# Values of the sample kept per pair of heads, and chunks of keys taken with a step

## The chip, the cores and the metric

The kernel runs on one core of a Trainium2 chip, as one launch. The metric is the device time of that launch in microseconds; of the kernel before there are three timed runs, 959.19, 959.48 and 960.69 us, and their median, 959.48 us, is the time that counts. One more execution was profiled. All times inside the kernel come from that execution.

The engines are named as the profile names them: PE multiplies matrices, PEld loads its weights (the stationary operand, one column after the other), DVE, ACT and POOL work on elements, SP issues nearly all DMAs. A DMA moves packets: runs of bytes that are contiguous on both sides.

## The reference

One encoder layer is applied to a prompt of 256 tokens and to a sample of 2048 tokens. The tokens are laid out as rows of 64 on a grid. Half of the layer is a neighbourhood attention with 8 heads of 64, the other half a Fourier mix; both are normalised, gated and projected.

```python
def encoder_layer(x, w_in, rpb, w_fourier, b_fourier, g_pre, g_na, g_f, w_out, g_post):
    h = rms_norm(x, g_pre)
    proj = h @ w_in
    q, k, v, z_a, u_f, z_f = jnp.split(proj, [...], axis=-1)
    y_a = neighbourhood_attention(q, k, v, rpb)
    y_f = fourier_mix(u_f, w_fourier, b_fourier)
    mixed = jnp.concatenate([rms_norm(y_a, g_na) * jax.nn.silu(z_a),
                             rms_norm(y_f, g_f) * jax.nn.silu(z_f)], axis=-1)
    out = mixed @ w_out
    return x + rms_norm(out, g_post)
```

In the attention a query sees 8 rows by 16 columns of keys around it (in the prompt, which has only 4 rows, all 4). Everything is float32.

## The kernel before

**Stages.** From 0 to about 548 us the projections run. Float32 products are made of three products of float32r halves (a high and a low part; the helper `mm3`, L163). From 548 to 600 us come the Fourier transform's small matrices. From 600 to 843 us runs the attention, mixed with the Fourier half of the output projection. From 843 us the attention half of the output projection runs over 18 tiles.

**Where v goes.** The values v come out of the projection as tiles of 128 tokens by 512 columns (8 heads of 64). `put_rows` (L359) stores a tile of the sample to `vN` in DRAM, which is indexed by half of the columns, grid row, column, and the 512 channels. `v_copy` (L366) copies parts of `vN` to the four tensors `vD`, one for each strip of 23, 31, 31 or 24 columns of keys (`KW`, L32), so that the keys of one strip and some neighbouring grid rows lie one behind the other. The prompt's values go to `vP` directly.

**The groups of the attention.** `G` (L1261) holds 36 groups: for each of 4 pairs of heads (`pr`) the prompt and then, for 4 bands of grid rows (`R`, with 11, 15, 15 and 12 rows of keys, `NR`) and two halves of the columns (`hc`), 256 queries in two tiles `b` of 128. Each tile has its own strip of keys, so n = rows times strip width keys: 253 to 465 in the sample, 160 in the prompt.

**A group's way.** `prep_v` (L1183) loads the values of the pair's two heads: it cuts the n keys into m chunks of z keys (m is 2 to 4), and puts key number j*z + p on partition p, chunk j, of the tile `v` ([128, 7, 128]). One DMA loads all chunks of a tile, or two where the last chunk is shorter than the memory behind it allows. z is rounded up to a multiple of 8. `scores` (L1211) makes the logits, `bias_max` (L1237) adds the bias and finds the maximum, `exps` (L1250) and `soft` (L1254) make probabilities `w`, [128 queries, 2 heads, n keys]. `transp` (L1571) turns them, chunk by chunk: the chunk of `w` is the stationary operand, the identity (128 columns) moves, and the result in `ptb` has keys on partitions. ACT and DVE copy `ptb` to `pt`. `pv` (L1586) multiplies `v` and `pt`, chunk by chunk, into one accumulator. The chunks' list, `g["ch"]`, has for each chunk its first key, its number of keys and its place in `v`.

**What sets the order.** The program's order is written by hand; each engine runs its instructions in that order. In step k of the loop at L1816, `scores` works on group k, `transp` and `pv` on group k - 1, `prep_v` (near the step's end) on group k + 1, and `prep` (its queries) on group k + 4. So the values loaded at the end of step k are read by `pv` near the end of step k + 2. SP issues DMAs in order, and each of them waits until the eighth before it has landed, since they take turns on eight semaphores.

**The instructions that matter here.** In one pass over the pairs, `transp` makes, per head, 3 tiles of 2 chunks, 11 of 3 and 4 of 4: 55 transposes. With 2 heads and 4 pairs these are 440. Their chunks have 80 to 128 columns, and the columns of one chunk lie one behind the other in `w`.

Of the kernel before, what the change touches and what calls it, by code (L numbers as in the profile page):

```python
# [10 lines left out]
F32 = mybir.dt.float32  # L11
# [19 lines left out]
K0 = (0, 4, 12, 20)  # L31
KW = (23, 31, 31, 24)  # L32
# [142 lines left out]
def build(tc, A, O):  # L175
    nc = tc.nc
# [3 lines left out]
    dr = es.enter_context(tc.tile_pool(name="dr", bufs=1, space=DRAM))  # L180
# [1 line left out]
    qD = dr.tile([4, 128, T], F32, name="qD")  # L182
    kD = dr.tile([4, 128, T], F32, name="kD")

    vD = [dr.tile([32, w, 512], F32, name="vD%d" % i) for i, w in enumerate(KW)]
    vP = dr.tile([2, 4, 40, 512], F32, name="vP")
    zD = dr.tile([2, 512, T], F32, name="zD")
    ZD = dr.tile([128, 16, 512], F32, name="ZD")
    uD = dr.tile([TP, 512], F32, name="uD")

    vN, uN = [dr.tile([2, 32, 32, 512], F32, name=n) for n in ("vN", "uN")]
    sD = dr.tile([5, 128, 4, 512], F32, name="sD")
    xD = dr.tile([7, 128, 4, 512], F32, name="xD")
    ivD = dr.tile([18, 128], F32, name="ivD")
# [5 lines left out]
    ident = cst.tile([128, 128], F32, name="ident")  # L200
# [24 lines left out]
    def mmt(n):  # L225
        x = mmc[0] % 5 > 2
        mmc[0] += 1
        return ps.tile([128, n], F32, tag="t" if x else "a", name="mm", bufs=2 if x else 3)
# [115 lines left out]
    def vu_out(m, c):  # L344
        s, b = PL[c]
        o = st.tile([128, 512], F32, tag="f", name=m + "o", bufs=3)
        x = row_tile(c)
        nc.scalar.activation(o, acc.pop((m, c)), AF.Copy, scale=invt[:, x:x + 1])
        if s is not None:
            put_rows(m, 0, b, s, o)  # L350
        elif m == "u":
            nc.sync.dma_start(uD[c * 128:c * 128 + 128, :], o)
        else:
            for r in range(4):
                nc.sync.dma_start(vP[c, r, 8 * c:8 * c + 32], o[32 * r:32 * r + 32])
                x = 24 * (1 - c)
                nc.sync.dma_start(vP[1 - c, r, 32 * c:32 * c + 8], o[32 * r + x:32 * r + x + 8])

    def put_rows(m, sg, b, s, o):  # L359
        r = 16 * sg + 4 * s  # L360
        nc.sync.dma_start((vN if m == "v" else uN)[b, r:r + 4].rearrange("r c e -> (r c) e"), o)


    VC = ((0, 0, 0, 23, 0), (1, 0, 8, 24, 0), (1, 1, 0, 7, 24), (2, 0, 24, 8, 0), (2, 1, 0, 23, 8), (3, 1, 8, 24, 0))

    def v_copy(i):  # L366
        x, b, c0, n, d0 = VC[i]
        nc.sync.dma_start(vD[x][:, d0:d0 + n], vN[b][:, c0:c0 + n])


    uu_ = {}
# [125 lines left out]
    def vu(sg, S, hooks):  # L497
# [7 lines left out]
        for i, (j, s) in enumerate(seq):  # L505
            for x in loads.get(i, ()):
                op_load(x)
            if i in splits:
                op_split(splits[i])
            for f in hooks.get(i, ()):  # L510
                f()
            p = mmt(512)
            h, l = op_[j]
            th, tl = bnew[sg, j]
            for k in range(4):
                mm3(nc, p, th[:, k, 128 * s:128 * s + 128], tl[:, k, 128 * s:128 * s + 128], h[k // 2][:, k % 2],
                    l[k // 2][:, k % 2], k == 0, k == 3)
            T2 = lambda o, a: nc.vector.tensor_tensor(out=o, in0=a, in1=p, op=ALU.add)
            if j == 0:
                uc[s] = et("uc")  # L520
                nc.scalar.copy(uc[s], p)
            elif j == 2:
                T2(uc[s], uc[s])
            elif j == 3:
                u4[s] = et("u4")
                T2(u4[s], uc[s])
            else:
                o = st.tile([128, 512], F32, tag="f", name="vuo", bufs=3)
                T2(o, (u4 if j in (4, 6) else uc)[s])
                if j == 4:  # L530
                    T2(uc[s], uc[s])
                put_rows("v" if j in (1, 6) else "u", sg, int(j in (4, 6)), s, o)
# [104 lines left out]
    for kp in range(4):  # L637
        ks = slice(2 * kp, 2 * kp + 2)
        v = part(RV[kp // 2], kp)
# [131 lines left out]
    for b in range(16):  # L771
# [13 lines left out]
        if 2 <= b < 8:  # L785
            x, y = divmod(b, 2)
# [9 lines left out]
        p = mmt(512)[:, :TP]  # L796
# [3 lines left out]
        o = st.tile([128, 256], F32, tag="f", name="f", bufs=3)  # L800
        if kind % 2:
            i, d = p, o
        else:
            i = p.rearrange("p (b r c) -> p b r c", b=2, c=32)
            d = o.rearrange("p (r b c) -> p b r c", b=2, c=32)
# [47 lines left out]
    for i in range(16):  # L853
        sg, pr = divmod(i, 8)
# [14 lines left out]
        o = [st.tile([128, 1024], F32, tag="f", name="f", bufs=3) for x in range(2)]  # L869
# [31 lines left out]
        for j in range(7):  # L901
            for f, d in ((u_load, 0), (u_split, 4), (u_stage1, 6)):
                x = 7 * pr + j - 7 - d
# [33 lines left out]
            if sg == 0:  # L937
                x, y = divmod(7 * (pr - 1) + j, 14)
# [27 lines left out]
            if 9 <= i < 15 and j == 2:  # L966
                v_copy(i - 9)
            p = mmt(512)
# [34 lines left out]
    ptb = [ps.tile([128, 512], F32, tag="t", name="ptb", bufs=2) for i in range(2)]  # L1003
# [179 lines left out]
    def prep_v(g):  # L1183
        cs = slice(g["pr"] * 128, g["pr"] * 128 + 128)
        g["v"] = jl.tile([128, 7, 128], F32, tag="v", name="v", bufs=VB)
        g["ch"], j = [], 0
        for b, (c0, w) in enumerate(g["t"]):
            n = g["nr"] * w
            src = (vP[b] if g["R"] is None else vD[2 * g["hc"] + b][K0[g["R"]]:]).rearrange("r c e -> (r c) e")
            m = -(-n // 128)  # L1190
            z = min(-(-n // m) + 7 & ~7, 128)
            f = m if src.shape[0] >= m * z else n // z
            nc.sync.dma_start(g["v"][:z, j:j + f], src[:z * f, cs].rearrange("(j p) e -> p j e", p=z))
            if f < m:
                nc.sync.dma_start(g["v"][:n - z * f, j + f], src[z * f:n, cs])
            ch = [(z * x, min(z, n - z * x), j + x) for x in range(m)]
            g["ch"].append(ch)
            j += len(ch)
        g["za"] = jl.tile([128, 256], F32, tag="za", name="za", bufs=VB)
        nc.sync.dma_start(g["za"], zD[1, cs, g["ts"]])  # L1200

# [69 lines left out]
    for g in G[:2]:  # L1271
        prep(g)
        prep_v(g)
# [11 lines left out]
    for t, (g, x) in enumerate(zip(G, (0, 640))):  # L1285
        g["w"] = []
        for c0, w in g["t"]:
            n = 2 * g["nr"] * w
# [282 lines left out]
    def transp(g, b):  # L1571
        ch = g["ch"][b]
        n, z = len(ch) * 128, ch[0][1]
        o = jp.tile([128, 2, 512], F32, tag="pt", name="pt", bufs=PB)
        for h in range(2):
            for j, (c0, nk, v) in enumerate(ch):
                nc.tensor.transpose(ptb[h][:nk, j * 128:j * 128 + 128], g["w"][b][:, h, c0:c0 + nk], ident)  # L1577
            if h == 0:
                nc.scalar.copy(o[:z, h, :n], ptb[h][:z, :n])  # L1579
            else:  # L1580
                V.tensor_copy(o[:z, h, :n], ptb[h][:z, :n])
        g["pt"] = g.get("pt", []) + [o]
# [109 lines left out]
    def part(P, name, n):  # L1692
        return [sm.tile([128, n, 128], F32R, tag="y%s%d" % (x, n) if n < 4 else "y" + x, name="y" + x,
                        bufs=3 if n == 4 else 1) for x in "hl"]
# [103 lines left out]
    prep(G[4])  # L1798
    f_mm(0)
    transp(G[0], 0)  # L1800
    f_norm(range(2))
    transp(G[0], 1)
    soft(G[1], 1)
    run_later()
# [4 lines left out]
    pv(G[0])  # L1809
    ys_load(ftiles[2])  # L1810
    prep_v(G[2])
    split_q(G[3])
    prep(G[5])
    ones32 = sm.tile([128, 32], F32, name="ones32", bufs=1)
    nc.vector.memset(ones32, 1.0)
    for k in range(2, len(G) + 1):  # L1816
        pr, i = divmod(k, 9)
        g, f = G[k] if k < len(G) else None, G[k - 1] if k else None
# [14 lines left out]
        if k == 28:  # L1833
            for c, x in enumerate(("kh", "kl")):
                w = kp.tile([128, T], F32R, tag=x, name="wk")
                WO[c] = [w[:, 56 + D * y:56 + D * y + D] for y in range(2)]
        if k in WK:
            c, y = WK[k]
# [3 lines left out]
        x = k // 2 + 1  # L1842
# [11 lines left out]
        if not g:  # L1854
            a_mm(atiles[0], 0, range(6))
        transp(f, 0)
        if g:
            exps(g, 0, 1)
# [57 lines left out]
        if k + 1 < len(G):  # L1916
            prep_v(G[k + 1])
# [123 lines left out]
```

## Time and profile before

| what | us |
|---|---|
| median of three runs | 959.48 |
| the profiled execution | 958.19 |
| its span, first to last instruction | 956.4 |
| PE busy | 944.8 |
| PEld busy | 784.3 |
| DVE busy | 732.0 |
| ACT busy | 505.8 |
| POOL busy | 453.3 |

The granted clock of PE was 0.997 of full speed. The DMA queue that SP feeds moved 270.68 MB. PE's matmuls overlap each other at their ends, so the durations of single matmuls are longer than the time from one to the next; how often they start is read from a row that merges several. A weight load overlaps the matmul before it.

### The profile page before, as it was taken

Reading aid. Unit: us, or ns where it says so; the run is one execution under the profiler, and the core shown is the slowest. Engines: PE = TensorE matmul, PEld = TensorE weight load, DVE = VectorE, ACT = ScalarE, POOL = GpSimd, SP = SyncE. Lnnn points to the kernel's source line nnn. Section 1 sums busy time; section 2 is a strip of 40 time slices with the busy share of each in tenths; the row PEclk is TensorE's granted clock in tenths of the full one; section 3 lists DMA queues with packets and bytes.
Section 4 is the critical chain, followed back from the end, with each engine's and each line's share of the span. In section 5 each row is a group of like instructions: output and inputs, shape, how many; then the busy total and the mean of one; then the engine's idle time right before and its main releaser. Section 6 shows DMA issues by size and latency. Waiting matters only on the chain.

```text
span 956.4 us, 16730 instructions
## 1 busy us (share of the span) xinstructions
PE 944.8 (99%) x5595; PEld 784.3 (82%) x5595; DVE 732.0 (77%) x1347; ACT 505.8 (53%) x1088; POOL 453.3 (47%) x426
## 2 busy tenths in 40 slices
PE   9999999999999999999999999999999999999996
PEld 7889988888888888888888879788787888788885
DVE  6758987788876765698887369777888878759876
ACT  6835676433334532233344267677876777654443
POOL 4100002464751302575566045567899798624444
PEclk9999999999999999999999999999999999999998
DMA  9899697557848894499889996698998999889995
GB/s 356 298 385 336 243 339 270 189 201 270 299 188 323 314 341 144 175 352 361 300 289 338 338 341 246 215 276 281 309 253 253 290 280 312 239 296 327 305 317 197
DMA packets 140790, 272.17 MB, mean 285 GB/s; under 512 B 12854, under 2 KB 80664, under 8 KB 137440
## 3 DMA queue, kind: packets, MB, share of 16 engines
q1 hardware_dynamic: 140352, 270.68, 82.9%
q8 instruction: 45, 0.74, 0.3%
q10 hardware_dynamic: 288, 0.40, 0.1%
q14 instruction: 41, 0.34, 0.1%
q0 software_dynamic: 64, 0.02, 0.0%
HBM read 181.37 MB, written 96.81 MB: 291 GB/s over the span
## 4 chain that ended last, share of the span: by engine, by line
PE 89%; DMA 4%; DVE 2%; POOL 2%; ACT 1%; issue 1%; SPq 0%; DVEq 0%; POOLq 0%; ACTq 0%
PE mm L166 18%; PE mm L164 18%; PE mm L165 18%; PE po L1504 10%; PE ptb L1577 5%; PE pv L1593 5%; PE s L1225 4%; DMA yr<-yD 2%; PE px L1689 2%; PE pz L1689 2%; DMA yo<-xt 1%; PE py L164 1%; PE py L165 1%; PE py L166 1%; PE ptb L1043 1%
## 5 line engine op out<-in xcount | busy, mean ns | idle before, releaser
L164 PE MATMUL mm<-xh,wa 128*128 128x512 f32 x448 | 174.4, 389 | 0.0
L166 PE MATMUL mm<-xh,wa 128*128 128x512 f32 x448 | 174.3, 389 | 0.0
L165 PE MATMUL mm<-xl,wa 128*128 128x512 f32 x448 | 174.3, 389 | 0.0
L545 POOL TENSOR_TENSOR ws<-wr 128x512 f32<-128x512 f32 x16 | 22.6, 1415 | 219.3 <-DMA wr<-wz 215.6
L1259 POOL TENSOR_SCALAR w<-w,m 128x465 f32<-128x465 f32 (+9 forms) x136 | 89.3, 670 | 32.7 <-DVE m L1256 13.5
L165 PEld LDWEIGHTS mm<-xl,wa 128*128 128x128 f32 x448 | 84.1, 188 | 17.5
L164 PEld LDWEIGHTS mm<-xh,wa 128*128 128x128 f32 x448 | 84.1, 188 | 17.5
L166 PEld LDWEIGHTS mm<-xh,wa 128*128 128x128 f32 x448 | 84.1, 188 | 17.4
L560 DVE TENSOR_TENSOR wa<-wr,wa 128x512 fp32r<-128x512 f32 x60 | 75.4, 1264 | 21.9 <-ACT wa L559 21.6
L1504 PE MATMUL po<-wk,yh 128*128 128x512 f32 x280 | 87.1, 392 | 0.9 <-ACT yh L1490 0.9
L1252 ACT ACTIVATE w<-w,m 128x465 f32<-128x465 f32 (+9 forms) x136 | 78.4, 579 | 14.3 <-DVE m L1247 13.6
L1968 POOL TENSOR_TENSOR xt<-of,xt 128x512 f32<-128x512 f32 x34 | 43.2, 1293 | 54.6 <-issue 33.0
L1247 DVE CUSTOM_DVE_ANT_1 w<-s,tb 128x465 f32<-128x465 f32 (+8 forms) x124 | 61.4, 529 | 8.9 <-PE s L1225 8.0
L598 POOL TENSOR_TENSOR mt<-mt,rmask 128x880 f32<-128x880 f32 (+2 forms) x24 | 50.3, 2111 | 32.6 <-DVE mt L594 26.2
L164 PE MATMUL mm<-vh,xh 128*128 128x512 f32 x168 | 65.4, 389 | 0.0
L165 PE MATMUL mm<-vl,xh 128*128 128x512 f32 x168 | 65.4, 389 | 0.0
L166 PE MATMUL mm<-vh,xl 128*128 128x512 f32 x168 | 65.4, 389 | 0.0
L1504 PEld LDWEIGHTS po<-wk,yh 128*128 128x128 f32 x280 | 52.1, 188 | 12.2 <-ACT yh L1490 1.3
L891 DVE TENSOR_TENSOR f<-u,mm 128x512 f32<-128x512 f32 x64 | 43.4, 679 | 23.3 <-PE mm L166 18.5
L1577 PE MATMUL ptb<-ident,w 128*120 128x128 f32 (+8 forms) x422 | 59.0, 277 | 1.4 <-ACT pt L1579 1.2
L559 ACT CAST wa<-wr 128x512 fp32r<-128x512 f32 x60 | 36.5, 618 | 43.5 <-PE mm L166 20.4
L1577 PEld LDWEIGHTS ptb<-ident,w 128*120 128x120 f32 (+8 forms) x422 | 47.1, 140 | 14.5 <-issue 4.6
(332 smaller groups left out, 2469.3 us busy)
## 6 DMA issues: line engine op xcount, KB each, us to landing
wr<-wz SPq DMA_DIRECT2D x48, 512.0 KB
vl<-sD SPq DMA_DIRECT2D x20, 512.0 KB
xm<-xm SPq DMA_DIRECT2D x9, 1024.0 KB
oD<-ofs SPq DMA_DIRECT2D x18, 512.0 KB
of<-oD SPq DMA_DIRECT2D x18, 512.0 KB
xt<-xn SPq DMA_DIRECT2D x18, 512.0 KB
yo<-xt SPq DMA_DIRECT2D x35, 256.0 KB
yr<-yD SPq DMA_DIRECT2D x34, 256.0 KB
```

What stands on the lines that cost most here:

```text
L164: nc.tensor.matmul(out, lh, rh, start=first, stop=False)
L165: nc.tensor.matmul(out, lh, rl, start=False, stop=False)
L166: nc.tensor.matmul(out, ll, rh, start=False, stop=last)
L560: nc.vector.tensor_tensor(out=o[:, 1], in0=src, in1=o[:, 0].bitcast(F32), op=ALU.subtract)
L598: nc.gpsimd.tensor_tensor(out=o, in0=i, in1=rmask[:, m0:m0 + n].unsqueeze(2).to_broadcast([128, n, 80]), op=ALU.add)
L891: nc.vector.tensor_tensor(out=dst(f, b), in0=src(uu[u]), in1=src(p), op=op)
L1247: nc.vector.tensor_tensor_reduce(out=rows(g["w"][b][:, h, :n], w), in0=rows(g["s"][2 * b + h][:, :nr * sw(w)], sw(w))[:, :, :w], in1=tv, s ...
L1252: nc.scalar.activation(w, w, AF.Exp, bias=m[:, h:h + 1], scale=-1.0, accum_out=m[:, 2 + h:3 + h])
L1259: nc.gpsimd.tensor_scalar(w, w, m[:, 4 + h:5 + h], 1.0, ALU.mult, ALU.mult)
L1504: nc.tensor.matmul(p, (d["l"] if x == 2 else d["h"])[:, c], w(n, int(x == 1), c), start=j == 0, stop=j == 11)
L1577: nc.tensor.transpose(ptb[h][:nk, j * 128:j * 128 + 128], g["w"][b][:, h, c0:c0 + nk], ident)
L1593: nc.tensor.matmul(p[hs, b], g["v"][:nk, v, hs], g["pt"][b][:nk, h, j * 128:j * 128 + 128], start=j == 0, stop=j == len(ch) - 1)
```

## The change

Four functions change, all for the sample's v; the prompt's `vP` keeps its layout, its loads take two neighbouring keys to one partition.

- `vN` and `vD` have the pair of heads as an outer index: the 128 channels of a pair are contiguous, and so are those of consecutive keys.
- `put_rows` stores a v tile with four runs of 512 bytes for each token where it was one of 2048.
- `v_copy` copies 128 runs (4 pairs, 32 rows) where it copied 32, each a quarter as long.
- `prep_v` puts m consecutive keys on each partition: key p*m + j goes to partition p, chunk j. A partition's m keys are one run of m times 512 bytes. z is n/m rounded up to a whole number, no longer to a multiple of 8, and there is one DMA a tile. Chunk x now holds the keys x, x + m, x + 2m and so on.
- `transp` takes as stationary operand every m-th column of `w`, beginning at x.

```diff
-    vD = [dr.tile([32, w, 512], F32, name="vD%d" % i) for i, w in enumerate(KW)]
+    vD = [dr.tile([4, 32, w, 128], F32, name="vD%d" % i) for i, w in enumerate(KW)]
...
-    vN, uN = [dr.tile([2, 32, 32, 512], F32, name=n) for n in ("vN", "uN")]
+    vN = dr.tile([2, 4, 32, 32, 128], F32, name="vN")
+    uN = dr.tile([2, 32, 32, 512], F32, name="uN")
...
     def put_rows(m, sg, b, s, o):
         r = 16 * sg + 4 * s
-        nc.sync.dma_start((vN if m == "v" else uN)[b, r:r + 4].rearrange("r c e -> (r c) e"), o)
+        if m == "v":
+            nc.sync.dma_start(vN[b, :, r:r + 4].rearrange("h r c e -> (r c) h e"), o.rearrange("p (h e) -> p h e", h=4))
+        else:
+            nc.sync.dma_start(uN[b, r:r + 4].rearrange("r c e -> (r c) e"), o)
...
-        nc.sync.dma_start(vD[x][:, d0:d0 + n], vN[b][:, c0:c0 + n])
+        nc.sync.dma_start(vD[x][:, :, d0:d0 + n], vN[b][:, :, c0:c0 + n])
...
             n = g["nr"] * w
-            src = (vP[b] if g["R"] is None else vD[2 * g["hc"] + b][K0[g["R"]]:]).rearrange("r c e -> (r c) e")
             m = -(-n // 128)
-            z = min(-(-n // m) + 7 & ~7, 128)
-            f = m if src.shape[0] >= m * z else n // z
-            nc.sync.dma_start(g["v"][:z, j:j + f], src[:z * f, cs].rearrange("(j p) e -> p j e", p=z))
-            if f < m:
-                nc.sync.dma_start(g["v"][:n - z * f, j + f], src[z * f:n, cs])
-            ch = [(z * x, min(z, n - z * x), j + x) for x in range(m)]
-            g["ch"].append(ch)
-            j += len(ch)
+            z = -(-n // m)
+            if g["R"] is None:
+                src = vP[b].rearrange("r c e -> (r c) e")
+                nc.sync.dma_start(g["v"][:z, j:j + m], src[:, cs].rearrange("(p j) e -> p j e", j=m))
+            else:
+                src = vD[2 * g["hc"] + b][g["pr"]].rearrange("r c e -> (r c) e")
+                k0 = K0[g["R"]] * w
+                nc.sync.dma_start(g["v"][:z, j:j + m], src[k0:k0 + z * m].rearrange("(p j) e -> p j e", j=m))
+            g["ch"].append([(slice(x, n, m), -(-(n - x) // m), j + x) for x in range(m)])
+            j += m
...
-                nc.tensor.transpose(ptb[h][:nk, j * 128:j * 128 + 128], g["w"][b][:, h, c0:c0 + nk], ident)
+                nc.tensor.transpose(ptb[h][:nk, j * 128:j * 128 + 128], g["w"][b][:, h, c0], ident)
```

On PE the transposes stay where they were, between the same matmuls; only their sizes change. These are the rows of PE in a step of the second band (`R` = 1, `hc` = 0), before and after. A row has the line, the operation, the tile written and those read (`w` is the chunk, `po` the output projection, `pn` a small transpose), the size of what is written, and how many of them follow each other.

```order
L1577 MATMUL ptb<-ident,w 120x128 x2
L1577 MATMUL ptb<-ident,w 105x128
L1577 MATMUL ptb<-ident,w 120x128 x2
L1577 MATMUL ptb<-ident,w 105x128
L1504 MATMUL po<-wo_5080,yh 128x512 x2
L1504 MATMUL po<-wo_5080,yl 128x512
L1504 MATMUL po<-wo_5081,yh 128x512 x2
L1504 MATMUL po<-wo_5081,yl 128x512
L1560 MATMUL pn<-ident,nsb 128x64
L1577 MATMUL ptb<-ident,w 120x128 x3
L1577 MATMUL ptb<-ident,w 105x128
```

```order
L1582 MATMUL ptb<-ident,w 115x128 x6
L1509 MATMUL po<-wo_5080,yh 128x512 x2
L1509 MATMUL po<-wo_5080,yl 128x512
L1509 MATMUL po<-wo_5081,yh 128x512 x2
L1509 MATMUL po<-wo_5081,yl 128x512
L1565 MATMUL pn<-ident,nsb 128x64
L1582 MATMUL ptb<-ident,w 117x128
L1582 MATMUL ptb<-ident,w 116x128 x3
```

Six transposes stay six (345 keys, a step of 3), eight stay eight (465 keys, a step of 4); the chunks of a tile are now equal to within one column.

On SP the loads of v keep their places, and the second loads of the last band go. These are SP's rows at the last band of the first pair (`R` = 3), before and after.

```order
L1193 DMA v<-vD_64 96x2x128
L1195 DMA v<-vD_64 84x128
L1193 DMA v<-vD_65 128x2x128
L1195 DMA v<-vD_65 116x128
L1200 DMA za<-zD 128x256
L1180 DMA ql<-qD 128x2x128
L1150 DMA tb<-tp 128x640
L1151 DMA tb<-tD_80 128x1760
```

```order
L1201 DMA v<-vD_64 92x384
L1201 DMA v<-vD_65 124x384
L1205 DMA za<-zD 128x256
L1184 DMA ql<-qD 128x2x128
L1154 DMA tb<-tp 128x640
L1155 DMA tb<-tD_80 128x1760
```

Four loads have become two, and what was 96 or 128 partitions with two separate runs of 512 bytes and a shorter rest is 92 or 124 partitions with one run of 1536 bytes.

## The prediction, made before the changed kernel was run

> **What bounds the kernel now.** I read the busy shares first, then the attention's stretches, then the chain of waits inside it, and last the groups of weight loads by shape. The first two views, one line and then one per stretch (length; busy us and count of PE, PEld, DVE, ACT, POOL; granted clock; DMA share; GB/s):
>
> ```profile
> PE 944.8 (99%) x5595; PEld 784.3 (82%) x5595; DVE 732.0 (77%) x1347; ACT 505.8 (53%) x1088; POOL 453.3 (47%) x426
> ```
>
> ```profile
> 400.00:500.00 100.00, 100.00 (x443) 82.81 (x442) 87.17 (x88) 36.66 (x65) 60.70 (x36) 1.00 0.90 317
> ...
> 670.00:735.00 65.00, 63.80 (x569) 51.43 (x568) 54.47 (x150) 49.25 (x135) 58.88 (x70) 1.00 0.94 270
> 735.00:795.00 60.00, 59.77 (x536) 48.62 (x534) 47.98 (x144) 44.36 (x126) 52.65 (x72) 1.00 0.99 292
> ...
> 843.00:956.00 113.00, 104.56 (x497) 85.91 (x493) 86.00 (x195) 48.20 (x138) 46.00 (x38) 0.98 0.87 291
> ```
>
> ```profile
> 600.00:843.00 243.00, 241.46 (x2153) 194.44 (x2151) 191.52 (x572) 178.19 (x508) 190.04 (x245) 1.00 0.92 270
> ```
>
> The change touches the attention, 600 to 843 us. There PE is busy for 241.46 of 243 us at full clock, while the DMA engines are busy 0.92 of the time. A full PE does not prove that DMAs are harmless, so the chain of waits comes next, here in a piece of the attention (start, length, what):
>
> ```profile
> by line: PE po L1504 34.5%; PE ptb L1577 22.2%; PE pv L1593 20.8%; PE s L1225 17.4%; PE ptb L1551 4.3%; PE pn L1560 1.3%
> ...
> 628.88 1.02 PE ptb L1577 x8
> 629.90 1.39 PE po L1504 x6
> 631.28 0.66 PE ptb L1577 x6
> ...
> 633.33 1.68 PE pv L1593 x28
> ...
> 636.72 0.80 PE ptb L1577 x6
> ...
> 641.27 1.69 PE pv L1593 x28
> ```
>
> In 619 to 660 us everything on the chain is PE, and the transposes (L1577) are 22.2% of it. So a nanosecond on a transpose is a nanosecond of the kernel here, and a faster load of v is nothing unless PE waits for it. What PEld waited for, 598 to 843 us (us, times, longest):
>
> ```profile
> PEld pv L1593 <- issue: 8.2, 24, 0.4
> PEld s L1225 <- issue: 5.8, 33, 0.2
> PEld ptb L1577 <- issue: 4.6, 18, 0.3
> PEld ptb L1577 <- POOL w L1259: 2.9, 7, 1.1
> PEld pv L1593 <- DVE dt L1444: 1.4, 4, 0.4
> ...
> PEld pv L1593 <- DMA tb<-tD: 0.4, 1, 0.4
> PEld pv L1593 <- DMA wk<-woD: 0.4, 1, 0.4
> ```
>
> No row names a load of v; all DMA rows together are 0.8 us.
>
> **What goes.** A v load's runs of 512 bytes become runs of 1 to 2 KB, and 12 second loads vanish from SP. That shortens DMAs which PE does not wait for: the loads of step k are read in step k + 2, and two rows of pv above lie 641.27 - 633.33 = 7.9 us apart, so a load has some 15 us. The most that can come back is PE's free time, 243 - 241.46 = 1.5 us; the cover is the matmuls, and I count 0.
>
> **What is added to the stores.** The stores of v (16 DMAs, four runs a token) and the copies (128 shorter runs each) have more packets for the same bytes. They run before 548 us, where PE is busy 100.00 of 100 us in the row above although the DMA share is 0.90. The cover again is PE's queue of matmuls. If it failed: the page gives 140352 packets that took 82.9% of 16 engines.
>
> ```profile
> q1 hardware_dynamic: 140352, 270.68, 82.9%
> ```
>
> That is 0.829 x 16 x 956.4 / 140352 = 0.090 us a packet on one engine, or 21.3 GB/s. 16 x 128 x 3 = 6144 more packets at that price are 35 us spread over 16 engines; an estimate, and too high, since these packets are a quarter of the mean size. I count 0, with 0 to 3 us for a store that comes late.
>
> **What is moved: the weight loads of 440 transposes.** This decides. The chunk of probabilities is PE's stationary operand; its columns were neighbours, now they lie 2, 3 or 4 floats apart. By the counts of the kernel, 6 + 33 + 16 chunks a head: 48 transposes get step 2, 264 step 3, 128 step 4. First, how often a transpose starts now: in the chain above eight take 1.02 us and six 0.80, so two more cost 0.22, or **0.11 us each** (six at 0.66 say the same). Is that the load or the matmul? Groups of weight loads by shape (count, busy us, mean ns of one):
>
> ```profile
> L1504 PEld LDWEIGHTS po<-wk,yl 128*128 128x128 f32 x140 | 26.3, 188 | 6.5 <-DVE yl L1495 1.1
> L1577 PEld LDWEIGHTS ptb<-ident,w 128*105 128x105 f32 x48 | 8.2, 171 | 0.0
> L1593 PEld LDWEIGHTS pv<-pt,v 105*64 105x64 f32 x96 | 6.2, 138 | 0.0
> L1577 PEld LDWEIGHTS ptb<-ident,w 128*128 128x128 f32 x38 | 4.8, 140 | 1.3
> L1577 PEld LDWEIGHTS ptb<-ident,w 128*80 128x80 f32 x24 | 2.5, 118 | 1.1 <-issue 0.4 <-POOL yr L1481 0.2
> L1577 PEld LDWEIGHTS ptb<-ident,w 128*101 128x101 f32 x14 | 2.3, 167 | 0.0
> L1034 PEld LDWEIGHTS pab<-d,zg 128*32 128x32 f32 x32 | 1.1, 146 | 0.3 <-issue 0.3
> L1551 PEld LDWEIGHTS ptb<-sqs,ones 128*32 128x32 f32 x32 | 0.8, 108 | 0.9 <-issue 0.5 <-DVE sqs L1889 0.3
> ```
>
> Contiguous loads come at three rates. A transpose's load of 80 columns takes 118 ns and of 128 takes 140: 0.46 ns a column. With odd counts, 101 and 105, it is 167 and 171: 1.0 ns a column. Ordinary loads (64 columns 138, 128 columns 188) are at 0.8. The rest is a fixed latency that the next load overlaps. At the slowest of these 128 columns would hold PEld for 0.13 us at most, and the odd chunks of 105 (0.105 us) fit inside 0.11; so today the 128 moving columns set the pace, not the load.
>
> One load in the trace has a step: L1034 takes every eighth column of `zg`, 32 columns, in 146 ns where 32 neighbours (L1551) take 108. And it shows how often such loads start:
>
> ```profile
> 553.74 0.57 PEld L1034 LDWEIGHTS pab<-d,zg 128*32 128x32 f32 x16 [0.17 <-issue]
> ```
>
> Sixteen go in pairs side by side; eight pairs in 0.57 us, the last lasting 0.146: (0.57 - 0.146) / 7 = 0.061 us a pair, **1.9 ns a column**, twice the ordinary rate. That a slow load does set the pace shows where the matmul is short, one moving column behind 128 loaded, 1.23 / 12 = 0.10 us each:
>
> ```profile
> 854.67 1.23 PE pna L1567 x12
> ```
>
> Now both ends. At 0.8 ns a column the largest chunk, 127, takes 0.10 us and hides under 0.11: nothing lost. At 1.9 ns:
> - step 4 (465 keys, 116.25 columns): 0.221 us, 0.111 more than 0.11, times 128 = **14.2 us**;
> - step 3 (mean 111 columns): 0.211, 0.101 more, times 264 = 26.7 us;
> - step 2 (mean 95.5): 0.181, 0.071 more, times 48 = 3.4 us.
>
> Between ends that far apart I take the nearest row for each step: step 4 is nearer, as a ratio, to the row with 8 (2 to 1) than to neighbours (4 to 1): 14.2 us. Steps 2 and 3 are, as a difference, far nearer to neighbours (1 and 2 against 6 and 5): 0. That choice is the weakest of the sum, so I checked it by interpolation between 0.8 and 1.9: if the rate grew evenly with the step, steps 3 and 4 would cost 1.11 and 1.27 ns a column, 3.5 + 4.8 = 8.3 us; if evenly with the step's logarithm, 1.38 and 1.53 ns, 11.4 + 8.7 = 20 us. 14.2 lies between. These transposes sit on the chain, so nothing hides their 14.2 us; they fall on PE in bands 1 and 2 of each pair.
>
> [...]
>
> **Sum.** 0 + 0 + 14.2 = 14.2 us on the profiled execution's 958.19 (span 956.4): 972.4. The median of the runs is 1.3 us above that execution, so I predict **973.7**.
>
> **Rivals.**
> 1. *Step 3 pays too.* For it: nothing in the trace tells 12 bytes from 32. Against: nothing tells it from neighbours either. If such columns cost 1.25 ns, between 0.8 and 1.9, a chunk of 111 takes 0.139 us, 0.029 more, times 264 = 7.6 us: 981. In full 26.7 more: 1000.
> 2. *The step costs nothing*, because a transpose's load starts from a faster rate (0.46 ns a column) and half of that is 0.92, still 0.107 us for 116 columns and under 0.11; or the change is done but the runs are split again. Time: 959 to 960. For it: the odd chunks, at half the fast rate, do hide. Against: L1034.
> 3. *Faster.* The same free loads, and the lighter DMA queues end the waits on DMAs: the 1.5 us of free PE time in the attention, and of the 113 - 104.56 = 8.4 us behind 843 a little, since stores left over from the attention no longer stand before its loads. It wins if the transposes' pace stays under 0.115 us (440 x 0.005 = 2.2 us would eat it up). Time: 957.
> 4. *Loads on few engines.* Chunks were multiples of 8 partitions; now 127, 117, 115 or 92. Suppose a load of 127 runs of 1 KB went through a single engine: 130 KB at 21.3 GB/s are 6.1 us instead of 0.4. It has some 15 us, but the queue behind it is in order and at 0.94 to 0.99. Three such loads (the first of the four is issued long before) at 0 to 6.1 us each: 0 to 18 on top; with 6, 980. No view of before shows how many engines a load uses.
>
>    [...]
>
> **How the numbers follow.** Forecast (step 4 alone) 0.38; rival 1 in part 0.18, in full 0.10; rival 2 0.17; rival 3 0.08; rival 4 0.09. The range leaves out rival 1 in full and most of rival 3: 958.0 to 992, which also holds the stores' 3 us. Within 0.2% (about what a measurement of this kernel can tell from no change) lies 957.6 to 961.4: rival 2 and a little of 3, 0.19. Faster 0.07, slower 0.74.
>
> **What would show it.** In the loads by shape, transposes of 116 and 117 columns well over 200 ns, and in the chain eight transposes of step 4 taking some 1.9 us where they took 1.02; six of step 3 still 0.66 to 0.80. PE's share stays 99%, and the attention gets 14 us longer while everything before 600 and after the attention keeps its length. If eight still take 1.02, rivals 2 or 3 hold; if six take 1.3, rival 1; if PEld's waits name v, rival 4. What would make me wrong altogether: waits on DMAs before 548 us.

## The result

| kernel | median, us | runs | against the kernel before (95% interval) |
|---|---|---|---|
| before | 959.48 | 5 | 1 |
| changed | 969.12 | 5 | 1.0106 (1.0087 to 1.0124) |

Two more runs of the kernel before were timed beside the changed kernel; its median stayed. The changed kernel is slower by 9.6 us, 1.1%. The prediction was 973.7, with a range of 958 to 992. The time lies within the range and on the forecast side. But the profile shows the loss in two places, and the prediction had put it in one.

The page of the changed kernel, PE's busy time and the DMA queue of SP:

```profile
PE 952.4 (99%) x5595; PEld 793.3 (82%) x5595; DVE 731.7 (76%) x1347; ACT 506.9 (52%) x1088; POOL 452.2 (47%) x426
...
q1 hardware_dynamic: 130232, 270.44, 81.1%
```

The DMA side did what the change says: 10120 packets fewer for nearly the same bytes (270.44 MB where it was 270.68). The span is 966.7 us where it was 956.4. Stages of the changed kernel (length; busy us and count of PE, PEld, DVE, ACT, POOL; granted clock; DMA share; GB/s):

```profile
400.00:500.00 100.00, 100.00 (x442) 82.79 (x442) 85.06 (x89) 36.85 (x65) 61.02 (x36) 1.00 0.91 314
...
548.00:600.00 52.00, 49.62 (x349) 40.95 (x348) 38.42 (x106) 34.68 (x70) 24.93 (x29) 1.00 0.77 271
600.00:843.00 243.00, 242.36 (x2069) 199.04 (x2068) 190.92 (x568) 176.63 (x501) 185.95 (x241) 1.00 0.85 265
```

The same view of the kernel before, for the one stretch that was not shown above:

```profile
548.00:600.00 52.00, 52.00 (x362) 43.66 (x361) 41.59 (x123) 37.72 (x80) 26.61 (x34) 1.00 0.83 296
```

Read the counts as well as the shares. Up to 548 us next to nothing differs. From 548 to 600 PE now idles for 52 - 49.62 = 2.38 us. From 600 to 843 it is as busy as before, yet in the same 243 us it does 84 matmuls fewer (2069 against 2153). So there is **a wait** ahead of the attention, and **slower work** inside it.

How much falls to which? The transposes of all groups but the first two, as the view of one line gives them (ns min/median/max, first and last start in us), in the changed kernel:

```profile
L1582 PEld LDWEIGHTS ptb<-ident,w x422: 151/186/376, 616.8 to 856.4; 128*116 128x116 f32 x32, 128*115 128x115 f32 x16, 128*120 128x120 f32 x16, 128*124 128x124 f32 x16
```

and in the kernel before:

```profile
L1577 PEld LDWEIGHTS ptb<-ident,w x422: 115/137/244, 613.6 to 847.1; 128*120 128x120 f32 x68, 128*105 128x105 f32 x17, 128*96 128x96 f32 x14, 128*128 128x128 f32 x14
```

The first starts 616.8 - 613.6 = 3.2 us later, the last 856.4 - 847.1 = 9.3 us later. So 3.2 us are lost ahead of the attention, 6.1 in it, and 1.0 of the span's 10.3 behind it. No run here shows what the last 1.0 comes from.

**The wait.** What ACT waited for from 560 to 600 us in the changed kernel (us in total, times, longest), and then in the kernel before:

```profile
ACT wo L1308 <- DMA wr<-wo: 5.0, 2, 4.8
```

```profile
ACT wo L1303 <- DMA wr<-wo: 0.4, 1, 0.4
```

`wr` are output weights. They have nothing to do with v, but their load stands behind two loads of v in SP's queue. ACT, waiting for them, does not evacuate PE's accumulators, and PE stops. (The profile books PE's own wait of 2.4 us as "issue"; that it stops for ACT is read from the order of the instructions, and from e2 below, where both waits go.) Why are the weights late? The rate of all DMAs from 560 to 590 us in the changed kernel, 40 slices of 0.75 us:

```profile
GB/s 418 386 451 416 428 331 311 217 120 43 91 307 241 289 365 299 293 263 329 397 392 400 386 274 108 85 37 23 25 1 98 44 251 393 448 415 448 382 437 437
```

Around 580 us it is 37, 23, 25: about what the prediction worked out for a single DMA engine (21.3 GB/s). From 580.5 to 581.75 us the trace holds 30 packets of 1 KB, one behind the other, which take 6.9% of 16 engines: about one engine has work, and the rest have none. The loads of v as SP's instructions (ns min/median/max) say the same, changed kernel and kernel before:

```profile
L1201 SPq DMA_DIRECT2D v<-vD x64: 248/332/6121, 562.0 to 838.9; - x64
```

```profile
L1193 SPq DMA_DIRECT2D v<-vD x64: 311/452/2680, 562.5 to 830.4; - x64
```

To issue one of these loads now holds SP for up to 6.1 us. The longest in each of the four pairs of heads (3.9, 6.1, 3.9 and 5.0 us) is the load right behind the one to 127 partitions. That is what rival 4 supposed, which the prediction gave 0.09.

**The slower work.** The weight loads of the transposes by shape in the changed kernel (count, busy us, mean ns of one):

```profile
L1582 PEld LDWEIGHTS ptb<-ident,w 128*116 128x116 f32 x96 | 16.5, 218 | 0.0
L1582 PEld LDWEIGHTS ptb<-ident,w 128*117 128x117 f32 x32 | 9.2, 289 | 2.8 <-issue 2.1 <-POOL w L1264 0.3
L1582 PEld LDWEIGHTS ptb<-ident,w 128*115 128x115 f32 x48 | 8.2, 243 | 1.9 <-issue 1.2 <-POOL w L1264 0.5 <-POOL ysum L1719 0.2
L1582 PEld LDWEIGHTS ptb<-ident,w 128*124 128x124 f32 x48 | 6.3, 192 | 0.7
L1582 PEld LDWEIGHTS ptb<-ident,w 128*120 128x120 f32 x48 | 6.2, 186 | 0.7
...
L1582 PEld LDWEIGHTS ptb<-ident,w 128*113 128x113 f32 x14 | 3.2, 231 | 0.0
```

With step 3, 115 columns take 243 ns and 124 columns only 192. With step 4, 117 take 289; 116 have a mean of 218, but one that follows another 116 takes 184 to 188 in the trace, and the mean also holds the loads that queue behind a 117. The step doesn't sort these rows. Odd and even do. This was not foreseen at all.

The timeline of PE (start, length from the first start to the last end) shows what that does to whole tiles of the changed kernel:

```profile
632.70 1.34 PE L1582 MATMUL ptb<-ident,w 128*117 128x128 f32 x8
...
624.28 1.21 PE L1582 MATMUL ptb<-ident,w 128*115 128x128 f32 x6
...
635.26 0.82 PE L1582 MATMUL ptb<-ident,w 128*120 128x128 f32 x6
```

The tile of step 4 (two chunks of 117, six of 116) is this one in the kernel before:

```profile
628.81 1.09 PE L1577 MATMUL ptb<-ident,w 128*120 128x128 f32 x8
```

It takes 0.25 us longer now. The six with step 3 and 120 columns fit into 0.82; the six with 115 take 1.21.

All transposes of a kernel can be added up from the records: for each run of them, from the start of the matmul before it to the start of the one behind (us; the columns on the right belong to experiments below).

```
tiles (transposes in each)        before  changed  e3_both  e7_contig
16 of 465 keys (8)                  18.0     20.4     18.4       18.0
24 of 341, 345 and 360 keys (6)     20.3     23.9     21.0       20.3
32 others                           25.5     26.1     26.4       25.5
sum                                 63.7     70.5     65.8       63.7
```

The transposes cost 6.8 us more than before: 2.5 for the 465 keys (20.45 - 17.99), 3.6 for the 341, 345 and 360, 0.7 for the rest. Within the second row the 3.6 us fall to the tiles of 341 and 345 keys, which have odd chunks (14.0 us before, 17.6 now); the tiles of 360 keys, in chunks of 120, take 6.3 us in both kernels.

### The profile page after: what moved, and what is told of

It is laid out like the page before. It is cut to its first block, busy times and chain, and to the rows that moved or that the text cites. A ratio compares the mean times of both kernels' runs of the same rounds, so it can differ in the third digit from the quotient of the medians.

```text
span 966.7 us, 16720 instructions
## 1 busy us (share of the span) xinstructions
PE 952.4 (99%) x5595; PEld 793.3 (82%) x5595; DVE 731.7 (76%) x1347; ACT 506.9 (52%) x1088; POOL 452.2 (47%) x426
## 3 DMA queue, kind: packets, MB, share of 16 engines
q1 hardware_dynamic: 130232, 270.44, 81.1%
## 5 line engine op out<-in xcount | busy, mean ns | idle before, releaser
L165 PEld LDWEIGHTS mm<-xl,wa 128*128 128x128 f32 x448 | 84.1, 188 | 17.6
L1582 PEld LDWEIGHTS ptb<-ident,w 128*116 128x116 f32 (+11 forms) x422 | 58.2, 205 | 11.9 <-issue 5.4
L1582 PE MATMUL ptb<-ident,w 128*116 128x128 f32 (+11 forms) x422 | 66.6, 294 | 0.5 <-ACT pt L1584 0.4
```

The costliest lines, as they stand in the source:

```text
L165: nc.tensor.matmul(out, lh, rl, start=False, stop=False)
```

## The experiments

Four theories stood against each other in pairs. For the transposes: A, odd or even decides; B, the step decides, as forecast. For the wait: C, loads on few engines; D, packets or order.

**e1: an even number of columns.** Behind the end of a tile's keys `w` has spare columns; an odd chunk reads one of them as well. The additional row of the result is never copied.

```diff
-                nc.tensor.transpose(ptb[h][:nk, j * 128:j * 128 + 128], g["w"][b][:, h, c0], ident)
+                e = nk + nk % 2 if True and g["w"][b].shape[2] in (360, 480) else nk
+                cols = slice(j, j + len(ch) * (e - 1) + 1, len(ch))
+                nc.tensor.transpose(ptb[h][:e, j * 128:j * 128 + 128], g["w"][b][:, h, cols], ident)
```

> The changed kernel, but a transpose that would load an odd number of strided columns (113, 115 or 117) loads one more column of the same step, which nobody uses; only the first two groups stay as they are. Theory A (the number of columns decides: a strided load of an even number of columns goes at about 0.9 ns a column and hides under the 0.109 us between transposes, an odd one goes at 1.4 ns with step 3 and 1.8 ns with step 4): the 32 loads of 117 columns save about 0.10 to 0.13 us each and the 64 of 115 and 113 about 0.05, together 6 to 7 us, so 962 to 963. Rival B (the step decides, as forecast: every load with step 4 pays for its step): one more column changes nothing, 969, or 0.1 us more.

Measured: 965.18 us, 1.0069 (1.0054 to 1.0085). The transposes load more columns and the kernel is 3.9 us faster than the changed one. The loads by shape:

```profile
L1584 PEld LDWEIGHTS ptb<-ident,w 128*116 128x116 f32 x144 | 18.9, 187 | 2.1 <-issue 1.2 <-POOL w L1264 0.5 <-POOL ysum L1721 0.2
...
L1584 PEld LDWEIGHTS ptb<-ident,w 128*118 128x118 f32 x32 | 6.0, 188 | 3.5 <-issue 1.8 <-POOL kl L1145 0.7 <-POOL w L1264 0.6
```

A column more, and a load falls from 289 to 188 ns, or from 243 to 187. A holds and B falls. The saving is smaller than the 6 to 7 us that A gave: the sum of the transposes falls from 70.5 to 65.8, so 4.7 us, and the time by 3.9.

**e2: v on all engines.** Loads go to multiples of 16 partitions.

```diff
-                nc.sync.dma_start(g["v"][:z, j:j + m], src[k0:k0 + z * m].rearrange("(p j) e -> p j e", j=m))
+                q = z + 15 & ~15
+                for a, e in ((0, q),) if k0 + q * m <= src.shape[0] else ((0, q - 16), (q - 16, z)):
+                    nc.sync.dma_start(g["v"][a:e, j:j + m], src[k0 + a * m:k0 + e * m].rearrange("(p j) e -> p j e", j=m))
```

> The changed kernel, but every load of v goes to a number of partitions that is a multiple of 16, by loading a few keys more than are used, or in two pieces where the tensor ends; the transposes are those of the changed kernel. Theory C (a load of 127 runs is served by one DMA engine and one of 114 by six; the DMAs behind it wait for those engines, and PE's idle time of 2.3 us at 580.8 us comes from there): the idle time goes and the kernel is 2.5 to 3.5 us shorter, 966. Rival D (the idle time comes from the smaller packets of the stores and copies, or from the order of issue): no change, 969.

Measured: 965.46 us, 1.0066 (1.0053 to 1.0079), 3.7 us less than the changed kernel. It loads more keys with 12 DMAs more, and it is faster. The stretch ahead of the attention:

```profile
548.00:600.00 52.00, 52.00 (x361) 43.59 (x360) 41.73 (x123) 37.62 (x80) 26.74 (x33) 1.00 0.82 296
```

PE's idle time is gone, and ACT's wait for `wr` is down from 5.0 to 0.3 us:

```profile
ACT wo L1310 <- DMA wr<-wo: 0.3, 1, 0.3
```

C holds, and the packet records of the changed kernel show the engines. From 566.3 to 567.9 us its only stream of 1 KB packets starts one every 0.042 us, one behind the other: the load to 127 partitions. The load right behind it, to 114 partitions, has 114 packets of 1536 bytes: 95 of them, five or six at a time, start from 567.28 to 569.20 us, and 19 more, one behind the other, from 572.26 to 573.61. That fits one engine for the load to 127, and for the one to 114 six engines with 19 packets each, of which one came 5 us late. D falls, since e2 leaves the packets of the stores and copies, and the order of issue, as they are.

**e3: both edits.**

> Both edits at once: even numbers of strided columns, and v loaded to multiples of 16 partitions. If theories A and C are the whole of it, the two savings add up: 969.1 - 6.5 - 3 = 959.6, within 1 us of the kernel before. If the lighter DMA queues are worth something once the losses are gone, it falls below the kernel before, 957 to 958. If something else in the change costs time (stores with shorter runs), it stays above 961.

Measured: 960.34 us, 1.0015 (1.0006 to 1.0023). The savings of e1 and e2 alone, 3.9 + 3.7 = 7.6, nearly make up the 8.8 us that go. Of the 9.6 us that the change cost, 8.8 are explained by two properties that its idea does not need: odd counts of strided columns, and loads to partition counts that are no multiple of 16.

**e4: the kernel before, with the changed kernel's chunk sizes.**

```diff
-            z = min(-(-n // m) + 7 & ~7, 128)
+            z = -(-n // m)
```

> The kernel before, with nothing changed but the number of keys in a chunk: the smallest that does, not rounded up to a multiple of 8 (127, 114, 115, 117, 92, 124 as in the changed kernel). Keys of a chunk stay neighbours, v keeps its layout and its runs of 512 bytes. Theory C: the loads to 127 and 114 partitions are late as in the changed kernel and the stall before the attention is there too, 961 to 963. Rival D: no change, 959.5. By theory A the odd contiguous loads (0.87 ns a column) still hide, so nothing on top.

Measured: 974.26 us, 1.0159 (1.0146 to 1.0172). C gave the direction, but the loss is 15 us and not 2 to 4. The stall ahead of the attention is there (48.76 us of PE in 548 to 600), and then PE waits inside the attention too:

```profile
PE pv L1593 <- DMA v<-vD: 6.5, 5, 3.0
```

The changed kernel has no such row. Beside the waits there is a second loss: right behind the longest of them, from 810.5 to 817.3 us, the granted clock is 0.50. Both kernels have the same partition counts; here a partition's keys are 2 to 4 packets of 512 bytes, there one packet of 1 to 2 KB. So the longer packets of the change seem to help where few engines serve a load: that is 974.3 with short packets against 965.2 with long ones and even transposes (e1). The two differ in the stores and copies as well, which e7 below finds to cost nothing that can be measured. The transposes read neighbouring columns here, odd ones too; 115 columns in a row take no longer than 0.11 us each (six start in 0.67 us).

**e5: steps and partition counts by themselves.** Behind the end of the kernel before stand these lines, then ordinary matmuls with 32 moving columns, and lines that load and copy `dv`.

```python
for st in (1, 2, 3, 4, 8):
    for nk in (116, 117):
        cols = slice(0, st * (nk - 1) + 1, st)
        for x in range(12):
            nc.tensor.transpose(tq[x % 2][:nk], tw[:, cols], ident)
```

> The kernel before, with a piece behind its end: 12 transposes for each step of 1, 2, 3, 4 and 8 floats and each of 116 and 117 columns (128 moving columns), 12 ordinary matmuls with 32 moving columns for steps 1, 4 and 8, and then loads of 1 KB a partition to 112 to 128 partitions, two each, one after another. Theory A (odd or even decides): the 116-column transposes start every 0.11 us with every step up to 4; the 117-column ones every 0.11 with steps 1 and 2, 0.16 with step 3 and 0.21 with step 4. Rival B (the step decides): 116 and 117 columns alike, both slow with step 4. Step 8: by A 0.11 with 116 columns, by B, from the 1.9 ns a column of the one strided load of the kernel before, 0.22. Theory C (engines): loads to 112 and 128 partitions take about 2 us from issue to the copy behind them; to 113 and 127 partitions, a prime number, 3 to 6 us more; to 114, 115 and 117 between. Rival D: all alike.

One run; its time (1023.23 us) is that of kernel and piece. PE's timeline of the piece, twelve transposes a row: step 2 with 117 columns, then 116 and 117 columns with step 3, with step 4, with step 8.

```profile
960.80 1.47 PE L2035 MATMUL tq<-ident,tw 128*117 128x128 f32 x12
...
962.11 1.47 PE L2035 MATMUL tq<-ident,tw 128*116 128x128 f32 x12
...
963.42 2.08 PE L2035 MATMUL tq<-ident,tw 128*117 128x128 f32 x12
...
965.34 1.47 PE L2035 MATMUL tq<-ident,tw 128*116 128x128 f32 x12
...
966.65 2.72 PE L2035 MATMUL tq<-ident,tw 128*117 128x128 f32 x12
...
969.21 1.47 PE L2035 MATMUL tq<-ident,tw 128*116 128x128 f32 x12
...
970.52 2.77 PE L2035 MATMUL tq<-ident,tw 128*117 128x128 f32 x12
```

From one row's start to the next, divided by 12: 116 columns 0.109 us with steps 3, 4 and 8; 117 columns 0.109 with step 2, 0.160 with step 3, 0.213 with step 4. With step 8, 117 columns start every 0.218 us in the records. A is right on every count that was taken at full clock, step 8 included. (Step 1 fell into a stretch at a granted clock of 0.50, and so did most of the ordinary matmuls; both are in e8.)

The loads of 1 KB a partition, one after another: DVE copies what has landed, and the bracket is what it waited since the copy before.

```profile
966.13 0.29 DVE L2047 COPY dz<-dv 117x256 f32<-117x256 f32 x1 [2.13 <-DMA dv<-vD]
...
975.41 0.29 DVE L2047 COPY dz<-dv 116x256 f32<-116x256 f32 x1 [3.08 <-DMA dv<-vD]
...
984.04 0.29 DVE L2047 COPY dz<-dv 114x256 f32<-114x256 f32 x1 [2.24 <-DMA dv<-vD]
...
1000.27 0.29 DVE L2047 COPY dz<-dv 113x256 f32<-113x256 f32 x1 [6.50 <-DMA dv<-vD]
1002.60 0.29 DVE L2047 COPY dz<-dv 112x256 f32<-112x256 f32 x1 [2.04 <-DMA dv<-vD]
...
1020.13 0.29 DVE L2047 COPY dz<-dv 127x256 f32<-127x256 f32 x1 [7.18 <-DMA dv<-vD]
```

112 partitions take 2.04 us, 114 take 2.24, 116 take 3.08, 117 take 2.13, 113 take 6.50 and 127 take 7.18. (A second load of each size took within 0.3 us of these.) At the 0.042 us that one engine took for a packet of 1 KB in the changed kernel, 113 packets one behind the other would take 4.7 us and 127 would take 5.3; 113 and 127 partitions took 4.5 and 5.1 us more than 112. By this estimate each of the two went through a single engine. C holds for them. How many engines served the other loads of this piece these rows do not show.

**e6: even columns with step 4 alone**, on top of e2 (in the diff of e1, only where a tile has four chunks).

> The changed kernel with v loaded to multiples of 16 partitions, and even numbers of columns in the transposes with step 4 alone; those with step 3 keep 113 and 115. By the sums of the groups' times in the traces (step 4: 20.4 us with 117 columns, 18.4 with 118) step 4 is worth 2.0 us: 965.5 - 2.0 = 963.5, and the rest of the 5.1 us between the kernel with v spread alone and the one with both edits belongs to step 3. If step 4 carried the loss, as forecast, it falls to 960.5 to 961.

Measured: 963.0 us, 1.0046 (1.0032 to 1.0061). From 965.46, 2.5 us go with step 4, and 2.7 more to e3 with step 3. The loss is shared about evenly between them (by the sums of the transposes 2.3 and 2.3); "step 4 alone" falls.

**e7: neighbouring columns, the rest as in e3.** This kernel leaves out that a chunk's probabilities belong to the keys in `v`: it times the loads, and its output is not the layer's.

```diff
-                cols = slice(j, j + len(ch) * (e - 1) + 1, len(ch))
+                cols = slice(j * z, j * z + e)
```

> The kernel with both edits, but each transpose reads neighbouring columns, as many of them as in the kernel with both edits, and even: the keys of the probabilities and of v no longer match, so the output is another one. Layout, stores, copies and loads of v are those of the kernel with both edits. What is left of the change is its DMAs alone. Theory E (an even strided load, 0.9 ns a column against 0.48, still costs where nothing lies ahead of it, the first of a group above all; by the traces' sums 65.8 against 63.7 us): 958.3 to 959. Rival F (the remaining 1.1 us over the kernel before come from the stores, or the loads): 960.3 as before.

Measured: 959.55 us, 1.0008 (0.9995 to 1.0020), the time of the kernel before. What is left of the change in this kernel, its stores, copies and loads, neither costs nor gains anything that can be measured. The loads of 116 columns:

```profile
L1586 PEld LDWEIGHTS ptb<-ident,w 128*116 128x116 f32 x144 | 16.3, 135 | 2.3 <-issue 1.2 <-POOL w L1266 0.5 <-POOL ysum L1723 0.2
```

135 ns where the strided ones take 187 in e1, and the sum of the transposes is that of before, 63.7. This speaks for E, but the intervals of e3 and e7 overlap, so whether the last microsecond of e3 is the strided loads isn't settled.

**e8: ordinary matmuls.** Is the price of an odd count a matter of transposes? The same piece with ordinary matmuls of the rounded type, and full-size matmuls ahead of each block (the granted clock is 1.00 over the rows below).

```python
nc.tensor.matmul(tq[x % 2][:nk, :128], tr[:, cols], tr[:, :128], start=True, stop=True)
```

> The kernel before with a piece behind its end that keeps PE's clock up: for each step of 1, 2, 3, 4 and 8 floats 12 ordinary matmuls (not transposes; the rounded type of the kernel's projections, 128 moving columns) with 116 and with 117 stationary columns, with full-size matmuls ahead of each block; last 12 transposes of 116 and 117 neighbouring columns. Question: is the price of an odd count a matter of transposes alone? If ordinary loads follow the same rule (theory A): 116 columns start every 0.10 us or less with every step, 117 every 0.16 with step 3 and 0.21 with steps 4 and 8. If the rule is one of transposes alone (rival G): 116 and 117 alike, 0.09 to 0.10 us up to the step at which the rate of the strided load in the kernel before (1.9 ns a column with step 8, 0.22 us) takes over. The transposes of neighbouring columns: 0.11 us each, odd or even.

One run (1002.34 us with the piece). PE's timeline for step 1 (116 and 117 columns), step 2 (117), step 3, step 4 and step 8 (116 and 117 each):

```profile
965.12 1.34 PE L2039 MATMUL tq<-tr 128*116 128x128 f32 x12
966.30 1.40 PE L2039 MATMUL tq<-tr 128*117 128x128 f32 x12
...
970.66 1.48 PE L2039 MATMUL tq<-tr 128*117 128x128 f32 x12
...
973.94 1.92 PE L2039 MATMUL tq<-tr 128*116 128x128 f32 x11
975.69 2.08 PE L2039 MATMUL tq<-tr 128*117 128x128 f32 x12
979.57 2.50 PE L2039 MATMUL tq<-tr 128*116 128x128 f32 x11
981.92 2.72 PE L2039 MATMUL tq<-tr 128*117 128x128 f32 x12
986.42 2.58 PE L2039 MATMUL tq<-tr 128*116 128x128 f32 x11
988.83 2.80 PE L2039 MATMUL tq<-tr 128*117 128x128 f32 x12
```

Odd and even are alike. From one start to the next within a row it is 0.102 us with step 1, 0.109 with step 2, 0.160 with step 3, 0.213 with step 4, 0.220 with step 8: 0.87, 0.93, 1.38, 1.83 and 1.88 ns a column. G holds. The type is not what sets the two apart: L1034, which the prediction shows, is an ordinary load of plain float32 with 32 columns, an even number, and it paid 1.9 ns a column. The last lines of the piece, 117 neighbouring columns in transposes, start every 0.109 us.

## Why the prediction was near, and which step of it failed

- **What bounds the kernel: right.** PE stays busy for 242.36 of 243 us. A microsecond on the transposes was roughly one of the kernel: their sum grew by 6.8 us and the attention by 6.1; in e1 the sum fell by 4.7 and the time by 3.9.
- **What goes (DMA relief, 0): right, as far as it shows.** e7 has the longer packets, the new stores and copies, and no strided load (but 12 second loads, from e2), and stands at 1.0008 (0.9995 to 1.0020). PE is busy there for 241.47 of 243 us from 600 to 843, as before: the 1.5 us of free time did not come back.
- **Stores and copies (0): right.** Up to 548 us the stages are the same, and e7 holds them too.
- **The weight loads: the right place and the right rates, for the wrong loads.** The step that failed is the price by step alone: step 4 at 1.9 ns a column for all 128 chunks, step 3 at nothing for all 264. Measured, an odd transpose costs 0.213 us with step 4 (forecast 0.221) and 0.160 with step 3 (rival 1 in part had 0.139). But only 32 of the 128 chunks with step 4 are odd (the 117s), and 64 of the 264 with step 3 (48 of 115, 16 of 113). With the measured paces 32 x 0.104 + 64 x 0.051 = 6.6 us; the records gave 6.8. That agreement is closer than it should be: even counts took back 4.7 us (e1), and the other 2.1, which by the records stay in e3 and go in e7, belong to strided loads as such. So the term of 14.2 was twice too large, and its split between the steps was wrong too. The choice behind it used two measures: step 4 was put to the row with step 8 by a ratio, step 3 to neighbouring columns by a difference. By the ratio step 3 would have gone to step 8 as well (8/3 against 3).
- **Why the trace of before could mislead.** The prediction saw that contiguous transposes load at 0.46 ns a column with even counts and 1.0 with odd ones, and took from it that both hide. It was the clue: odd counts load like ordinary ones. The price with a step was then taken from the one strided row, L1034, an ordinary matmul, and ordinary loads with step 4 come near the forecast (1.83 ns in e8; with step 3, which was put at nothing, they pay 1.38). Even transposes don't.
- **Rival 2 (0.17) had the mechanism of the even chunks.** It said that a transpose's load starts from 0.46 ns a column, and that at half that rate, 0.92, it still hides. 336 of the 440 chunks are even. Their strided loads of 116 columns take 187 ns where contiguous ones take 135 (e1, e7): 52 ns for 116 columns, so 0.45 ns a column more, 0.91 in all, and they start every 0.109 us. It failed on the 96 odd chunks with steps 3 and 4.
- **Rival 4 (0.09) came true beside the forecast.** "Loads on few engines" cost some 3 us by the trace (3.2 ahead of the attention) and 3.7 by e2. Its estimate of 6.1 us for a load of 127 through one engine was fair: 7.18 - 2.04 = 5.1 us more than a load to 112 partitions. But the mark was wrong: the waits do not name v. The loads of v had time; what stood behind them in the queue, `wr`, had not. (With the shorter packets of e4 the waits do name v.) That everything before 600 us keeps its length fell with it.
- The sum was near by luck: two errors met, 7 too much on the transposes, and 3 to 4 too little on the DMAs.

No version here beats the kernel before; e3 and e7 suggest why: on the side that the change lightens, nothing was won that could be measured.

## What to carry to other kernels

Before you put a step into a stationary operand, count its columns: a float32 transpose with an even number of them (116, with 128 moving columns) took steps up to 8 at full pace here, one with an odd number paid like an ordinary load from step 3 on, and one spare column took most of that price away. A load to 112 partitions took 2.04 us here and one to 113 took 6.50, so try DMAs at a multiple of 16 partitions, as e2 did for 3.7 us, and where that can't be, look at what stands behind it in the queue, since the wait appeared there here. And where a profile shows two rates for the same operation, find what sorts them before a rate is taken from another operation.

## What the runs showed of the hardware that was not expected

- A float32 transpose with an even number of stationary columns escapes the price of the step: 116 columns every 0.109 us with steps 3, 4 and 8 (that the 128 moving columns set this pace is the prediction's estimate); 117 columns 0.160 and 0.213 with steps 3 and 4.
- A slow DMA blocks more than its own data: right behind a load to 127 partitions, SP was held for up to 6.1 us in the issue of the next load of v (at most 2.1 in e2), and in e4, with shorter packets, for up to 9.1:

```profile
L1193 SPq DMA_DIRECT2D v<-vD x64: 238/817/9060, 561.5 to 851.0; - x64
```
